# A decoder step on one core: side pieces held until a PSUM bank is free, memory attention in two passes over the tokens, a new order in the first stage

## The chip, the core and the metric

The kernel runs on one core of a Trainium2 chip. TensorE (PE in the profile) multiplies, VectorE (DVE) and ScalarE (ACT) work elementwise, GpSimd (POOL) does small copies and sums, SyncE (SP) issues the DMAs. The metric is the device time of one execution in microseconds, as a median over runs. A change of 0.2% is about 2.5 us here.

## What is computed

One layer of a hybrid decoder, for 512 prompt tokens and 8 x 4 = 32 sample tokens, 544 in all, with the same weights. Model width is 1024. Everything is kept transposed: a tile is 128 channels by 544 tokens.

```python
u = rmsnorm(h, norm_mix)
qa, ka, va, qkv_b, z_b, beta, a, gate_a, gate_b = split(u @ w_in)
o_a = dilated_attention(qa, ka, va, caches)        # three groups of 4 heads, keys by stride
o_b = gated_deltanet(qkv_b, z_b, beta, a, state)   # 8 heads of 128, a chain over chunks
h += (sigmoid(gate_a) * (o_a @ w_branch_a) + sigmoid(gate_b) * (o_b @ w_branch_b)) @ w_out
# memory attention: 4 heads of 128, 256 memory tokens; the sample tokens have caches of their own
q = rmsnorm(h, norm_mem_q) @ w_mem_q
h += softmax(q @ mem_k.T / sqrt(128)) @ mem_v @ w_mem_o
gate, up = split(rmsnorm(h, norm_ffn) @ w_up)
h += (silu(causal_dwconv3(gate) + b) * up) @ w_down
y = rmsnorm(h, norm_final)
```

The caches and states, shifted by the new tokens, are outputs too.

## The kernel before

**Dense blocks.** All weights are cut into blocks of 128 x 1024 floats (512 KB), in the order that `plan()` gives: `dq`, `dk`, `dv` (dilated attention), `z`, `gq`... (DeltaNet), `gb`, `ga` (gates), `mk`, `mv` (memory keys and values), then `wa` and `bb` (the two branches), `wo`, four `mq` (queries into the memory, one head each), four `mo`, and the FFN's `fg`, `fu`, `fd`. `load_to` loads a block into one of three buffers `wr`. `split_to` splits it into a high and a low part, `wh` by ACT and `wl` by DVE, in two buffers each, so that a block's split waits until the last block but one has been used. The tokens are split in the same manner (`xh`, `xl` in the first stage, then `uh`/`ul`, `obh`/`obl`, `nh`/`nl`, `oh`/`ol`). `dense` multiplies a block by eight such tiles: for each of eight slices k three products (`wh` by high, `wh` by low, `wl` by high), each as two matmuls of 272 tokens, into one of two wide PSUM tiles `pd`.

**Side pieces.** All other work (attention, the DeltaNet chain, convolutions, softmax) is written as Python generators, called streams, that use four small PSUM banks (`b`). After each slice k `dense` calls `tick`, which may put the next piece of a stream into the program at that place. There is one program order for each engine, and every engine works strictly in it: a piece whose input is late holds everything behind it on its engine. The builder keeps an account: estimated costs of every instruction, and from them a time at which each engine, tile and bank would be done. `tick` takes the stream of highest priority whose input is ready by the account. `need` and `drain` force pieces in where a dense block needs their result.

**The first stage.** `start` loads the first weight block, the parameters `par` and eight tiles `x`; ACT and DVE split each (`xh`, `xl`) and, in between, sum squares. `first` runs `dq` and `dk` on the unscaled tokens, then makes the tokens' RMS factor (`rstd`: matmuls with ones, a square root on ACT, a reciprocal on DVE; `spread`: matmuls that spread it over the partitions into `rx`), evacuates both products by DVE, and runs `dv`, while ACT and DVE make the scaled tokens `uh`, `ul`.

**Merge.** `merge` multiplies the dilated branch (`wa`) and then the DeltaNet branch (`bb`). The first two `bb` blocks are first run over heads 0 to 5, and then over heads 6 and 7, which come last out of the chain.

**Memory attention.** `cross` runs the four `mq` blocks over all 544 tokens. After each it adds a stream `cross_head` (scores of the prompt tokens, softmax, transposes, values), and writes `cross_keys` straight into the program: the sample tokens' scores against cached keys `mks`, summed in `csc`. After the last block `cross_sample` (softmax of `csc`, product with the cached values `mvs`) and what is left of the streams follow with no dense block between. `mem_out` then runs `mo`, and the FFN follows.

All calls reach the hardware through one helper, so every instruction has the same line in the profile (L329). Tiles tell the work apart.

Of the kernel before, what the change touches and what calls it, by code (L numbers as in the profile page):

```python
# [111 lines left out]
def plan():  # L112

    blocks = []
    for kind, k in MIX:
        if kind == "mem":
            blocks += [("mk", h) for h in range(4)] + [("mv", q) for q in range(4)]
            continue
        blocks += [(kind + c, k) for c in "qkv"] if kind in "gd" else [(kind, k)]
    blocks += [("wa", m) for m in range(2)] + [("bb", m) for m in range(8)]  # L120
    blocks += [("wo", m) for m in range(8)]
    blocks += [("mq", h) for h in range(4)]
    blocks += [("mo", q) for q in range(4)]
    for s in range(0, KF, SEC):
        for j in range(s, min(s + SEC, KF)):
            blocks += [("fg", j), ("fu", j)]
        blocks += [("fd", (s, m)) for m in range(8)]
    return blocks


def _layout(i):
# [10 lines left out]
    def blk(name, key):  # L142
# [22 lines left out]
        if name == "mq":  # L165
            return _tiles(wmq, [128 * key])[0]
# [70 lines left out]
class _View:  # L237
# [17 lines left out]
    def __getattr__(self, name):  # L255
        return getattr(self.raw, name)

# [135 lines left out]
class Builder:  # L393
# [123 lines left out]
    def split_to(self, j):  # L517
        while self.next_split <= min(j, len(self.plan) - 1):
# [8 lines left out]
            hi = self.wp.tile([128, c], F32R, name=f"wh{n}", tag="wh", bufs=NHL)  # L527
            lo = self.wp.tile([128, c], F32R, name=f"wl{n}", tag="wl", bufs=NHL)
            self.acc.rotate("wh", NHL, _key(hi))
            self.acc.rotate("wl", NHL, _key(lo))  # L530
# [3 lines left out]
            self.hl.pop(n - NHL, None)  # L534
# [98 lines left out]
    def tick(self):  # L633
# [4 lines left out]
        while c["PE"] - t0 < PE_SHARE:  # L638
            runs = self.runnable()
            for n in sorted(range(len(runs)), key=lambda n: (runs[n]["prio"], runs[n]["ready"])):  # L640
                st = runs[n]
                lag = max(c["V"], c["A"]) - c["PE"]
                if st["ready"] <= c["PE"] and self.room(st, [a + b for a, b in zip((MAIN, 0), self.older(runs, n))]) and lag < LAG[st["prio"]] and c["P"] - c["PE"] < 6.0:
# [77 lines left out]
    def start(self):  # L721
# [12 lines left out]
        x = [self.s(name="x") for _ in range(KD)]  # L734
        self.load(out=x[0], in_=I["xT"][:, 0, :])
        for k in range(1, KD):
            self.load(out=x[k], in_=I["xT"][:, k, :])
# [7 lines left out]
        def square(k):  # L745
# [4 lines left out]
        self.split_to(0)  # L750
        for k in range(KD):
            g = self.p("g_mix", k)
            xh.append(self.s(dt=F32R, name="xh")), xl.append(self.s(dt=F32R, name="xl"))
            self.split_scaled(x[k], g, xh[k], xl[k])
            if k == 7:
                self.split_to(1)
            if k % 2:
                square(k // 2)
        for k in range(KD // 2, KD):
            square(k)  # L760
        return x, list(zip(xh, xl)), acc

    def first(self, t, x, xs, acc):

# [4 lines left out]
        def stat(k):  # L769
            if k == 5:  # L770
                r5.append(self.rstd([acc], N))
            if k == 7:
                self.spread(r5[0], N, r)
        pk = self.dense(("dk", t), xs, each=stat)
        del acc
        tl = [self.dil_evac(t, 0, pq, r), self.dil_evac(t, 1, pk, r)]
        self.uh, self.ul = [], []
        us = {}
# [6 lines left out]
        scale(0)  # L785

        def chain(k):
            scale(k + 1)
            self.split_x(us.pop(k), self.uh, self.ul)
        ps = self.dense(("dv", t), xs, each=chain)  # L790
        del xs
        tl.append(self.dil_evac(t, 2, ps, r))
        self.dil_done(t, tl)
# [754 lines left out]
    def dil_tiles(self, t):  # L1548
        us = list(zip(self.uh, self.ul))
        self.dil_done(t, [self.dil_evac(t, kind, self.dense((name, t), us)) for kind, name in enumerate(("dq", "dk", "dv"))])  # L1550
# [129 lines left out]
    def dil_sample(self):  # L1680
# [109 lines left out]
        yield 1, 0, 2, 0  # L1790
# [32 lines left out]
        v.tensor_tensor(o, o, acc[:, None, :].to_broadcast([128, 2, 64]), OP.add)  # L1823
        yield from self.wait(("ap", 0), ("ap", 1))
# [26 lines left out]
    def merge(self):  # L1851
# [28 lines left out]
        for lo, hi in ((0, HFIRST), (HFIRST, 8)):  # L1880
            xs = heads(lo, hi)
            for m in range(2):
                ps[m] = self.dense(("bb", m), xs, k0=lo, ps=ps.get(m), start=lo == 0, stop=hi == 8, ahead=m == (hi == 8))
# [14 lines left out]
    def out_proj(self):  # L1898
# [10 lines left out]
        for m in range(8):  # L1909
# [9 lines left out]
            self.hstat(m, "g_mq")  # L1919
# [6 lines left out]
    def hstat(self, m, gain, eng=None):  # L1926
# [7 lines left out]
        if m < 7:  # L1934
# [8 lines left out]
        if m == 7:  # L1943
            split()


    def cross(self):
        nc = self.nc
        v, act, mm = nc.vector, nc.scalar.activation, nc.tensor.matmul
        ident = self.cst("ident")  # L1950
        xs = list(zip(self.nh, self.nl))
        self.oh, self.ol = [None] * 4, [None] * 4
        r = None
        for h in range(4):
            if r is None:
                r = []
                ps = self.dense(("mq", h), xs, mid=lambda: r.append(self.rstd([self.hacc], N)))
                r = self.spread(r[0], N, self.s(name="rq"))
            else:
                ps = self.dense(("mq", h), xs)  # L1960
                self.cross_keys(h - 1)
            q = self.s(name="cq")
            v.scalar_tensor_tensor(q, self.dv(ps), 128.0 ** -0.5, r, op0=OP.mult, op1=OP.mult)
            dst = self.qm[:, 0:4]
            dst = bass.AP(tensor=dst.tensor, offset=dst.offset + 264 * h, ap=[list(dst.ap[0]), [132, 2], [32, 4], [1, 4]])
            nc.gpsimd.tensor_copy(dst, q[:, 512:544].rearrange("p (c s j) -> p s c j", c=4, s=2))
            self.oh[h], self.ol[h] = self.s(dt=F32R, name="oh"), self.s(dt=F32R, name="ol")
            self.add(self.cross_head(h, q), 1, (3, 0), (4, 0))
            del q
        self.cross_keys(3)  # L1970
        self.cross_sample()
        self.drain()

    def cross_load(self, n):

        for e in range(n, n + 2):
# [3 lines left out]
            elif e < 16:  # L1980
                b = (0, 2, 4, 6, 1, 3, 5, 7)[e - 8]
                self.mvs[b] = self.l((128, 1024), name="mvs")
                self.load(out=self.mvs[b], in_=self.I["mvs"][b])

    def cross_begin(self):
# [4 lines left out]
        self.mks, self.mvs = {}, {}  # L1990
        self.cross_load(0), self.cross_load(2), self.cross_load(4)

    def cross_keys(self, h):
# [15 lines left out]
        self.cross_load(6 + 2 * h)  # L2009
# [14 lines left out]
    def cross_head(self, h, q):  # L2024
# [3 lines left out]
        pt = [self.s((128, 512), name="cpt") for _ in range(2)]  # L2028
        ps = []
        for i in range(2):  # L2030
            pb = self.bank()
            for e in range(2):
                mm(pb[:, 256 * e:256 * e + 256], q[:, 256 * i + 128 * e:256 * i + 128 * e + 128], self.mkT[h], start=True, stop=True)
            ps.append(self.soft(pb))
            if i == 0:
                yield "at", 0.0, (1, 0, 1, 0)
        del q
        yield 0, 0
        for i in range(2):
            p, pb = ps.pop(0), self.bank()  # L2040
            for e in range(2):
                for j in range(2):
                    nc.tensor.transpose(pb[:, 256 * e + 128 * j:256 * e + 128 * j + 128], p[:, 256 * j + 128 * e:256 * j + 128 * e + 128], ident)
            act(pt[0][:, 256 * i:256 * i + 256], pb[:, 0:256], AF.Copy)
            v.tensor_copy(pt[1][:, 256 * i:256 * i + 256], pb[:, 256:512])
            del p
        yield
        pb = self.bank()
        for e in range(2):
            mm(pb, self.mvT[e][:, 128 * h:128 * h + 128], pt[e], start=(e == 0), stop=(e == 1))  # L2050
        act(self.oh[h][:, 0:512], pb, AF.Copy)
        v.tensor_tensor(self.ol[h][:, 0:512], pb, self.oh[h][:, 0:512].bitcast(F32), OP.subtract)
        yield

    def cross_sample(self):
# [3 lines left out]
        mvs = self.mvs  # L2059
        p = self.soft(self.csc, 1)  # L2060
        self.csc = None
        self.tick()
# [5 lines left out]
        self.tick()  # L2068
        self.tick()

        po, ot = self.wide(), self.l((128, 1024), name="ot")
        for s in range(2):
            for e in range(2):
# [266 lines left out]
```

## Time and profile before

| | |
|---|---|
| median of 3 runs | 1270.43 us (1270.27 to 1271.31) |
| profiled execution | 1269.83 us, its span 1268.1 us |
| PE busy | 1222.2 us, 96% of the span |
| DVE, ACT, POOL busy | 709.4, 526.6, 160.9 us |
| mean granted TensorE clock | 0.988 |
| DMA | 233.56 MB, 184 GB/s mean |

The span runs from the first to the last instruction; 1.7 us of the time lie around it. PE is busy nearly all the time, so the questions are how long it is idle, where, and where its clock is lower than full. In rows of the timeline the columns are start, duration, engine, operation, tiles, shape, count, and in brackets the idle time before and what ended it. "x2" is a pair of matmuls; their durations overlap, so the pace is read from one start to the next.

### The profile page before, as it was taken

Reading aid. Unit: us, or ns where it says so; the run is one execution under the profiler, and the core shown is the slowest. Engines: PE = TensorE matmul, PEld = TensorE weight load, DVE = VectorE, ACT = ScalarE, POOL = GpSimd, SP = SyncE. Lnnn points to the kernel's source line nnn. Section 1 sums busy time; section 2 is a strip of 40 time slices with the busy share of each in tenths; the row PEclk is TensorE's granted clock in tenths of the full one; section 3 lists DMA queues with packets and bytes.
Section 4 is the critical chain, followed back from the end, with each engine's and each line's share of the span. In section 5 each row is a group of like instructions: output and inputs, shape, how many; then the busy total and the mean of one; then the engine's idle time right before and its main releaser. Section 6 shows DMA issues by size and latency. Waiting matters only on the chain.

```text
span 1268.1 us, 25946 instructions
## 1 busy us (share of the span) xinstructions
PE 1222.2 (96%) x10482; PEld 1165.2 (92%) x10482; DVE 709.4 (56%) x1343; ACT 526.6 (42%) x1115; POOL 160.9 (13%) x356
## 2 busy tenths in 40 slices
PE   7999999999999999998999999799999999999997
PEld 6899988899999988998799998499999999999997
DVE  6535346666767974486566555364553355434564
ACT  6334434555645533665642234254332233312341
POOL 0000100211152130020000000021210022101110
PEclk9999999999999998999998999899999999999998
DMA  6332774653576568656564483545555555555422
GB/s 224 95 122 79 279 265 155 214 174 100 178 267 215 200 215 295 199 190 193 175 219 143 166 325 110 191 171 186 193 187 183 183 189 206 203 184 183 157 83 71
DMA packets 90117, 233.56 MB, mean 184 GB/s; under 512 B 25865, under 2 KB 31478, under 8 KB 89221
## 3 DMA queue, kind: packets, MB, share of 16 engines
q1 hardware_dynamic: 89998, 231.90, 53.1%
q8 instruction: 83, 1.36, 0.4%
q14 instruction: 36, 0.29, 0.1%
HBM read 198.42 MB, written 77.58 MB: 218 GB/s over the span
## 4 chain that ended last, share of the span: by engine, by line
PE 71%; DVE 5%; ACT 2%; issue 2%; DMA 1%; POOL 0%; DVEq 0%; POOLq 0%; SPq 0%; ACTq 0%
PE pd L329 58%; PE b L329 13%; DVE wl L329 1%; DVE y L329 1%; ACT wh L329 1%; DMA qk<-park 0%; DVE xr L329 0%; DMA ft<-park 0%; DVE sz L329 0%; DVE m L329 0%; DMA mvs<-in_mvs 0%; DVE st L329 0%; DMA z<-park 0%; ACT hsq L329 0%; DVE su L329 0%
## 5 line engine op out<-in xcount | busy, mean ns | idle before, releaser
L329 DVE TENSOR_TENSOR wl<-wr,wh 128x1024 fp32r<-128x1024 f32 (+2 forms) x174 | 212.4, 1223 | 225.2 <-ACT wh L329 219.1
L329 ACT ACTIVATE wh<-wr 128x1024 fp32r<-128x1024 f32 (+2 forms) x174 | 177.1, 1021 | 122.7 <-PE pd L329 120.5
L329 PE MATMUL pd<-uh,wh 128*128 128x272 f32 x1024 | 223.5, 300 | 0.0
L329 PE MATMUL pd<-ul,wh 128*128 128x272 f32 x1024 | 212.7, 289 | 0.4 <-DVE ul L329 0.3
L329 PE MATMUL pd<-uh,wl 128*128 128x272 f32 x1024 | 212.3, 288 | 0.0
L329 PEld LDWEIGHTS pd<-uh,wh 128*128 128x128 f32 x1024 | 160.2, 189 | 7.7 <-issue 6.4
L329 PEld LDWEIGHTS pd<-ul,wh 128*128 128x128 f32 x1024 | 162.1, 189 | 0.9 <-DVE ul L329 0.8
L329 PE MATMUL pd<-nh,wh 128*128 128x272 f32 x768 | 161.6, 291 | 0.5 <-DVE xr L329 0.5
L329 PEld LDWEIGHTS pd<-uh,wl 128*128 128x128 f32 x1024 | 161.8, 188 | 0.0
L329 PE MATMUL pd<-nh,wl 128*128 128x272 f32 x768 | 159.4, 288 | 0.0
L329 PE MATMUL pd<-nl,wh 128*128 128x272 f32 x768 | 159.3, 288 | 0.0
L329 PEld LDWEIGHTS pd<-nh,wh 128*128 128x128 f32 x768 | 121.9, 188 | 2.3 <-issue 2.0
L329 PEld LDWEIGHTS pd<-nl,wh 128*128 128x128 f32 x768 | 121.7, 188 | 0.0
L329 PEld LDWEIGHTS pd<-nh,wl 128*128 128x128 f32 x768 | 121.6, 188 | 0.0
L329 POOL TENSOR_TENSOR sr<-fy,rf 128x512 f32<-128x512 f32 (+1 forms) x44 | 53.5, 1237 | 69.5 <-ACT fy L329 66.3
L329 DVE SCALAR_TENSOR_TENSOR y<-cb,par,y 128x568 f32<-128x568 f32 x72 | 58.9, 820 | 2.9 <-ACT y L329 1.1
L329 PE MATMUL pd<-fh,wh 128*128 128x272 f32 x256 | 53.2, 288 | 0.0
L329 PE MATMUL pd<-fl,wh 128*128 128x272 f32 x256 | 53.1, 288 | 0.0
L329 PE MATMUL pd<-fh,wl 128*128 128x272 f32 x256 | 53.1, 288 | 0.0
L329 DVE SCALAR_TENSOR_TENSOR fy<-fcb,par,fy 128x560 f32<-128x560 f32 x44 | 35.3, 802 | 22.4 <-ACT fy L329 21.7
L329 PEld LDWEIGHTS pd<-fh,wl 128*128 128x128 f32 x256 | 40.6, 188 | 0.0
L329 PEld LDWEIGHTS pd<-fh,wh 128*128 128x128 f32 x256 | 40.5, 188 | 0.0
(371 smaller groups left out, 2121.0 us busy)
## 6 DMA issues: line engine op xcount, KB each, us to landing
wr<-in_w SPq DMA_DIRECT2D x145, 512.0 KB
out_d<-in_c SPq DMA_DIRECT2D x32, 1022.0 KB
ft<-park SPq DMA_DIRECT2D x40, 256.0 KB
kc<-in_ck SPq DMA_DIRECT2D x18, 512.0 KB
kc<-in_cv SPq DMA_DIRECT2D x18, 512.0 KB
wr<-in_wd SPq DMA_DIRECT2D x16, 512.0 KB
out_d<-in_c SPq DMA_DIRECT2D x8, 1016.0 KB
park<-y SPq DMA_DIRECT2D x24, 256.0 KB
```

The source lines that it names most:

```text
L329: return f(*a, **k)
```

## The change

1. `tick` starts a piece only when, by the account, the bank that it will take is free as well.
2. Memory attention goes in two passes over the tokens: first tokens 256 to 543 (288, with the sample tokens) for all four heads, then tokens 0 to 255. `part` runs one block over such a range. Blocks `mq` 0 and 1 are loaded and split a second time (as `mq` 4 and 5). `cross_head` works on 256 tokens at a time; `cross_keys` and `cross_sample` become one stream with priority 0, so that its pieces too lie between dense slices; `mo` begins with the second range for two output tiles.
3. The first stage: `x` 0 is loaded first and the first weight block in two halves; squares come after all splits; `dv` goes into two small banks; `rstd` comes after `dk`, `spread` after two slices of `dv`, and a fourth block (`dq` of tile 2) still runs on the unscaled tokens.
4. `merge` splits a third `bb` block ahead, into two large slots; before the last `wo` tile's statistics the second `mq` block is split; two pieces of the sample attention end where DVE has work to do (`yield "at", self.acc.done`).

The core of the diff:

```diff
@@ tick
-                if st["ready"] <= c["PE"] and self.room(...) and ...:
+                if max(st["ready"], self.acc.last.get(self.ring["b"][-4], 0.0) - 0.0 if len(self.ring["b"]) >= 4 else 0.0) <= c["PE"] and self.room(...) and ...:
@@ start
-        self.load_to(0)
+        x = [self.s(name="x") for _ in range(KD)]
+        w0 = [self.s((128, 512), name="w0") for _ in range(2)]
+        self.load(out=x[0], in_=I["xT"][:, 0, :])
         self.load(out=self.par, in_=I["par"])
+        for e in range(2):
+            self.load(out=w0[e], in_=self.src[0][:, 512 * e:512 * e + 512])
+            for k in range(2 * e + 1, 5 * e + 3):
+                self.load(out=x[k], in_=I["xT"][:, k, :])
...
+        piece(0)
+        for k in range(KD):
...
+            self.split_scaled(x[k], g, xh[k], xl[k])
+            if k == 2:
+                piece(1)
+        self.split_to(1)
+        for k in range(KD):
             sq = self.s(name="xsq") if k else acc
             act(sq, x[k], AF.Square)
@@ first
         def stat(k):
-            if k == 5:
+            if k == 7:
                 r5.append(self.rstd([acc], N))
-            if k == 7:
-                self.spread(r5[0], N, r)
         pk = self.dense(("dk", t), xs, each=stat)
...
+            if k == 1:
+                self.spread(r5[0], N, r)
+                tl.append(self.dil_evac(t, 0, pq, r))
+                tl.append(self.dil_evac(t, 1, pk, r))
+                scale(0)
...
+        pv = [self.bank((128, NH)) for _ in range(2)]
...
+        p2 = self.dense(("dq", t2), xs, each=more)
@@ merge
-                ps[m] = self.dense(("bb", m), xs, ..., ahead=m == (hi == 8))
+                ps[m] = self.dense(("bb", m), xs, ..., ahead=lo == 0 or m == 1)
@@ new
+    def part(self, b, xs, ps, cols, k0=0, ahead=True, last=True, mid=None):
+        self.reserve(2)
+        hi, lo = self.weights(b, ahead)
+        for k, (xh, xl) in enumerate(xs):
+            w = slice((k0 + k) * 128, (k0 + k + 1) * 128)
+            for n, (w, x) in enumerate(((hi[:, w], xh), (hi[:, w], xl), (lo[:, w], xh))):
+                self.nc.tensor.matmul(ps, w, x[:, cols], ...)
+            if mid and k == len(xs) - 3:
+                mid()
+            if k % 2:
+                self.tick()
@@ cross
-            self.add(self.cross_head(h, q), 1, (3, 0), (4, 0))
-        self.cross_keys(3)
-        self.cross_sample()
-        self.drain()
+        self.add(self.cross_sample(), 0, (0, 0), (3, 0))
...
+        for h in range(4):
+            half = self.bank((128, 288)) if h < 2 else self.wide()[:, 0:288]
+            self.part(("mq", h), xs, half, slice(256, N), ...)
+            todo.append((h, half))
+            if h == 1:
+                r[0] = self.spread(r[0], N, self.s(name="rq"))
+            while h and todo:
+                evac(*todo.pop(0))
+        for n, h in enumerate((2, 3, 0, 1)):
+            half = self.wide()[:, 0:256] if n < 3 else self.bank((128, 256))
+            self.part(("mq", h + 4 if h < 2 else h), xs, half, slice(0, 256), ahead=n > 0)
+            query(h, 0, half)
@@ cross_sample (now with yields between its pieces)
+        for h in range(4):
+            yield from self.wait(("cq", h))
+            yield from self.on(self.mks[2 * h], self.mks[2 * h + 1], need=(2 if h == 3 else 0, 0))
+            self.cross_keys(h)
+            yield 1, 0, 3, 0
...
+            yield from self.on(*[x for c in range(4) for x in mvs[2 * c + s]])
@@ mem_out
+        ps = [self.wide() for _ in range(2)]
+        for i in (1, 0):
+            self.need(*[("oh", h, i) for h in range(4)], *[("os", 0)] * i)
+            for m in range(2):
+                self.part(("mo", 0), xs, ps[m][:, 512:800] if i else ps[m][:, 256:512], ...)
```

What it moves, at three places. Names are tiles with running numbers, and x4 is a count of equal instructions.

The first place is the start of the program. SyncE's queue of loads before, and then after the change (`w_91` and `w_92` are the two halves of the first weight block that `wr_83` was):

```order
L329 DMA wr_83<-in_w 128x1024
L329 DMA par<-in_par 128x293
L329 DMA x_87<-in_xT 128x544
L329 DMA x_88<-in_xT 128x544
L329 DMA x_89<-in_xT 128x544
```

```order
L339 DMA x_83<-in_xT 128x544
L339 DMA par<-in_par 128x293
L339 DMA w_91<-in_w 128x512
L339 DMA x_84<-in_xT 128x544
L339 DMA x_85<-in_xT 128x544
L339 DMA w_92<-in_w 128x512
L339 DMA x_86<-in_xT 128x544
```

The first token tile and half a block now come ahead of the other half. Later in the same stage, on PE, where `spread` stands (`b_303`, `b_309` before; `b_329`, `b_335` after), between the last matmuls of `dk` (`pd_243`) and the first of `dv` (`pd_327`) before:

```order
L329 MATMUL pd_243<-xh_151,wl_158 128x272 x2
L329 MATMUL b_303<-ident,m_288 128x128 x4
L329 MATMUL b_309<-ident,m_288 128x32
L329 MATMUL pd_327<-xh_116,wh_239 128x272 x2
L329 MATMUL pd_327<-xl_117,wh_239 128x272 x2
```

and inside `dv` (now in the banks `b_315` and `b_316`) after:

```order
L339 MATMUL b_316<-xl_121,wh_245 128x272
L339 MATMUL b_315<-xh_120,wl_246 128x272
L339 MATMUL b_316<-xh_120,wl_246 128x272
L339 MATMUL b_329<-ident,m_306 128x128 x4
L339 MATMUL b_335<-ident,m_306 128x32
L339 MATMUL b_315<-xh_124,wh_245 128x272
```

`dv` no longer takes the wide tile that `dq`'s product still holds.

The second place is the merge, on PE: the last transposes of the DeltaNet heads (`b<-ident,ft`) against the products of heads 6 and 7. Before, heads 6 and 7 of the first `bb` block (`pd_8766`) follow the transposes at once:

```order
L329 MATMUL pd_8816<-obh_8756,wh_8762 128x272 x2
L329 MATMUL pd_8816<-obl_8757,wh_8762 128x272 x2
L329 MATMUL pd_8816<-obh_8756,wl_8763 128x272 x2
L329 MATMUL b_8883<-ident,ft_8445 128x128 x4
L329 MATMUL b_8894<-ident,ft_8555 128x128 x4
L329 MATMUL pd_8766<-obh_8901,wh_8640 128x272 x2
L329 MATMUL pd_8766<-obl_8902,wh_8640 128x272 x2
```

After, the first of the two transposes stands ahead of the second `bb` block (`pd_8865`), and the other stands four slices later:

```order
L339 MATMUL pd_8808<-obh_8777,wl_8744 128x272 x2
L339 MATMUL b_8853<-ident,ft_8402 128x128 x4
L339 MATMUL pd_8865<-obh_8274,wh_8804 128x272 x2
L339 MATMUL pd_8865<-obl_8275,wh_8804 128x272 x2
L339 MATMUL pd_8865<-obh_8274,wl_8805 128x272 x2
```

The chain that feeds these transposes ended among the `bb` blocks before; it now ends among the `wa` blocks.

The third place is the end of the memory attention, on PE (`cq` are queries, `mkv` the memory keys and values, `cp` softmax rows, `cpt` their transposes, `ot` the sample result). Before, after the 16 products with `mvs`:

```order
L329 MATMUL b_10376<-mkv_9600,cq_10307 128x256 x2
L329 MATMUL pd_10388<-ident,ot_10353 128x128 x8
L329 MATMUL b_10405<-cpt_10211,mkv_9601 128x512
L329 MATMUL b_10405<-cpt_10212,mkv_9602 128x512
L329 MATMUL b_10410<-ident,cp_10345 128x128 x4
L329 MATMUL b_10417<-ident,cp_10381 128x128 x4
L329 MATMUL b_10424<-cpt_10338,mkv_9601 128x512
L329 MATMUL b_10424<-cpt_10339,mkv_9602 128x512
L329 MATMUL pd_10435<-oh_9956,wh_10200 128x272 x2
```

After, between the second range of `mo` (the first row) and its first range (the last rows):

```order
L339 MATMUL pd_10455<-oh_10134,wl_10400 128x288
L339 MATMUL b_10480<-cpt_10437,mkv_9608 128x256
L339 MATMUL b_10480<-cpt_10437,mkv_9609 128x256
L339 MATMUL b_10485<-ident,cp_10445 128x128 x4
L339 MATMUL b_10493<-mkv_9606,cq_10452 128x256 x2
L339 MATMUL b_10505<-cpt_10490,mkv_9608 128x256
L339 MATMUL b_10505<-cpt_10490,mkv_9609 128x256
L339 MATMUL b_10510<-ident,cp_10498 128x128 x4
L339 MATMUL b_10518<-cpt_10515,mkv_9608 128x256
L339 MATMUL b_10518<-cpt_10515,mkv_9609 128x256
L339 MATMUL pd_10454<-oh_9970,wh_10399 128x256
L339 MATMUL pd_10454<-ol_9971,wh_10399 128x256
```

The products with `mvs` have moved ahead, in between the slices of the second `mq` pass; the scores of the last head, their softmax and the two products behind them still follow each other here.

More of the change, by code (lines that the diff above doesn't have):

```diff
@@ L121, in plan @@
     blocks += [("wo", m) for m in range(8)]
-    blocks += [("mq", h) for h in range(4)]
+    blocks += [("mq", h) for h in range(6)]
     blocks += [("mo", q) for q in range(4)]
@@ L165, in blk @@
         if name == "mq":
[L166 removed]
+            return _tiles(wmq, [128 * (key % 4)])[0]
         if name == "mo":
@@ L784, in scale, with more @@
                 x[k] = None
-        scale(0)
         def chain(k):
-            scale(k + 1)
-            self.split_x(us.pop(k), self.uh, self.ul)
-        ps = self.dense(("dv", t), xs, each=chain)
+            if k == 1:
[3 more added lines that the diff above has]
+                scale(0)
+            elif k % 2:
+                scale(k // 2)
+                self.split_x(us.pop(k // 2 - 1), self.uh, self.ul)
+        hi, lo = self.weights(("dv", t))
+        pv = [self.bank((128, NH)) for _ in range(2)]
+        for k in range(KD):
+            w = slice(128 * k, 128 * k + 128)
+            for n, (w, x_) in enumerate(((hi[:, w], xs[k][0]), (hi[:, w], xs[k][1]), (lo[:, w], xs[k][0]))):
+                for e in range(2):
+                    nc.tensor.matmul(pv[e], w, x_[:, NH * e:NH * e + NH], start=(k == 0 and n == 0), stop=(k == KD - 1 and n == 2))
+            chain(k)
+        dv = self.s(name="dv")
+        for e in range(2):
+            nc.vector.tensor_tensor(dv[:, NH * e:NH * e + NH], pv[e], r[:, NH * e:NH * e + NH], OP.mult)
+        self.store(out=self.O["dkv"][1, t], in_=dv[:, 0:512])
+        tl.append(dv)
+        del pv, dv
+        self.dil_done(t, tl)
+        t2 = t + 2
+        def more(k):
+            if k < 5:
+                e = 3 + k
+                scale(e + 1)
+                self.split_x(us.pop(e), self.uh, self.ul)
+        p2 = self.dense(("dq", t2), xs, each=more)
         del xs
-        tl.append(self.dil_evac(t, 2, ps, r))
-        self.dil_done(t, tl)
+        return self.dil_evac(t2, 0, p2, r)
     def mem_stream(self):
@@ L1546, in sample_bias, with dil_tiles @@
         return t
-    def dil_tiles(self, t):
+    def dil_tiles(self, t, q=None):
         us = list(zip(self.uh, self.ul))
-        self.dil_done(t, [self.dil_evac(t, kind, self.dense((name, t), us)) for kind, name in enumerate(("dq", "dk", "dv"))])
+        tl = [q] if q is not None else []
+        for kind, name in list(enumerate(("dq", "dk", "dv")))[len(tl):]:
+            tl.append(self.dil_evac(t, kind, self.dense((name, t), us)))
+        self.dil_done(t, tl)
     def dil_evac(self, t, kind, ps, r=None):
@@ L1882, in merge @@
             for m in range(2):
-                ps[m] = self.dense(("bb", m), xs, k0=lo, ps=ps.get(m), start=lo == 0, stop=hi == 8, ahead=m == (hi == 8))
+                ps[m] = self.dense(("bb", m), xs, k0=lo, ps=ps.get(m), start=lo == 0, stop=hi == 8, ahead=lo == 0 or m == 1)
         obs = heads(0, 8)
@@ L1947, in cross @@
     def cross(self):
-        nc = self.nc
-        v, act, mm = nc.vector, nc.scalar.activation, nc.tensor.matmul
-        ident = self.cst("ident")
+        v = self.nc.vector
         xs = list(zip(self.nh, self.nl))
         self.oh, self.ol = [None] * 4, [None] * 4
[L1953 to L1963, printed above, removed]
+        self.add(self.cross_sample(), 0, (0, 0), (3, 0))
@@ new lines, in query @@
+        def query(h, i, ps):
+            q = self.s((128, 256), name="cq")
+            v.scalar_tensor_tensor(q, ps[:, 0:256], 128.0 ** -0.5, r[0][:, 256 * i:256 * i + 256], op0=OP.mult, op1=OP.mult)
+            self.add(self.cross_head(h, i, q), 1, (2, 0), (2, 0))
+        todo = []
+        for h in range(4):
+            half = self.bank((128, 288)) if h < 2 else self.wide()[:, 0:288]
+            self.part(("mq", h), xs, half, slice(256, N), ahead=h < 3, mid=(lambda: r.append(self.rstd([self.hacc], N))) if h == 1 else None)
+            todo.append((h, half))
[3 more added lines that the diff above has]
+                evac(*todo.pop(0))
```

203 lines of the change are left out of this document (117 added, 86 removed).

## The prediction

> **What bounds the kernel now.** I read the page first, then busy time by stage, then what PE waited for, then single rows.
>
> ```profile
> span 1268.1 us, 25946 instructions
> PE 1222.2 (96%) x10482; PEld 1165.2 (92%) x10482; DVE 709.4 (56%) x1343; ACT 526.6 (42%) x1115; POOL 160.9 (13%) x356
> PE 71%; DVE 5%; ACT 2%; issue 2%; DMA 1%; POOL 0%; DVEq 0%; POOLq 0%; SPq 0%; ACTq 0%
> ```
>
> PE carries the span and 71% of the chain that ended last. The change removes no PE work: by the program's order it issues the same products, in other shapes. So only two things can move the time: PE's idle time, 1268.1 - 1222.2 = 45.9 us, and time in which PE works at a lower clock. Busy time by stage (columns: stretch, length, busy time and count of PE, PEld, DVE, ACT, POOL, granted clock, DMA share, GB/s):
>
> ```profile
> 0.00:39.20 39.20, 29.32 (x208) 28.09 (x208) 28.21 (x43) 23.41 (x35) 0.62 (x6) 1.00 0.52 185
> 39.20:560.00 520.80, 512.25 (x4880) 481.50 (x4879) 312.83 (x716) 250.20 (x637) 78.16 (x197) 0.99 0.58 195
> 560.00:670.00 110.00, 100.59 (x902) 92.41 (x901) 71.29 (x171) 59.69 (x161) 7.54 (x11) 0.97 0.58 192
> 759.20:825.40 66.20, 57.76 (x399) 42.80 (x398) 29.80 (x66) 22.69 (x62) 1.77 (x4) 0.95 0.45 166
> 825.40:850.90 25.50, 25.12 (x194) 24.46 (x192) 15.98 (x18) 12.18 (x17) 6.91 (x5) 1.00 0.41 151
> 850.90:1220.00 369.10, 368.86 (x2915) 368.89 (x2915) 175.33 (x214) 115.60 (x136) 65.86 (x133) 1.00 0.52 184
> ```
>
> The last row is the FFN: PE is busy in all of it, so nothing is to be had there. The idle time lies in the first stage (9.9 us), in the DeltaNet phase (8.6), from the memory keys to the merge (9.4) and in the memory attention, `mq` to `mo` (8.4 + 0.4). What PE waited for, in total, times and longest:
>
> ```profile
> PE pd L329 <- ACT xh L329: 7.4, 1, 7.4
> PE b L329 <- DVE sz L329: 2.8, 6, 0.8
> PE b L329 <- DVE cp L329: 2.3, 1, 2.3
> PE b L329 <- DVE ft L329: 2.0, 1, 2.0
> PE b L329 <- DVE ssc L329: 1.9, 1, 1.9
> PE pd L329 <- DVE dq L329: 1.9, 1, 1.9
> PE b L329 <- ACT cpt L329: 1.7, 1, 1.7
> PE pd L329 <- DMA mvs<-in_mvs: 1.7, 1, 1.7
> PE b L329 <- POOL qm L329: 1.4, 1, 1.4
> PE pd L329 <- DVE obl L329: 1.3, 1, 1.3
> PE b L329 <- DVE so L329: 0.8, 1, 0.8
> ```
>
> Each is a wait of one or two microseconds at a place where a piece follows too soon on what it needs. They cost more than their length. Four stretches around such places, and pairs of matmuls shortly after the merge's waits and later:
>
> ```profile
> 468.00:485.00 17.00, 13.60 (x159) 9.72 (x159) 10.66 (x19) 2.34 (x10) 2.58 (x3) 0.84 0.73 227
> 668.00:680.00 12.00, 11.23 (x69) 10.98 (x70) 7.63 (x11) 3.98 (x5) 0.00 (x0) 0.75 0.30 106
> 800.00:807.00 7.00, 3.24 (x41) 1.75 (x40) 3.27 (x8) 1.69 (x5) 0.21 (x1) 1.00 0.75 237
> 807.00:814.00 7.00, 5.03 (x25) 0.83 (x23) 1.48 (x4) 1.66 (x6) 0.00 (x0) 0.75 0.63 235
> ...
> 669.85 0.66 PE L329 MATMUL pd<-obh,wh 128*128 128x272 f32 x2
> 670.30 0.65 PE L329 MATMUL pd<-obl,wh 128*128 128x272 f32 x2
> 674.41 0.42 PE L329 MATMUL pd<-obl,wh 128*128 128x272 f32 x2
> 674.66 0.41 PE L329 MATMUL pd<-obh,wl 128*128 128x272 f32 x2
> ```
>
> After the merge's waits a pair takes 0.45 us (669.85 to 670.30), later 0.25 (674.41 to 674.66). The granted clock says the same: 0.75 over 12 us is 3.0 us of clock lost. In the memory attention PE is busy for 3.24 of 7 us, and the clock of the next 7 us is 0.75; over `mq` to the last side piece 0.95 of 66.2 us is 3.3 us lost. Around 476 us it is 0.16 x 17 = 2.7.
>
> The Trainium skill ("TensorE: Matmul & The Clock Gate", "What's actually happening") puts the return to the half clock after at least one idle window of about 3.4 us. The longest single wait after the start is 2.3 us here, and the clock fell all the same; the trace decides, and by that rule alone the waits would bring their own length and no more, which is a rival below.
>
> **The change, part by part.** The sum is made against the profiled execution, 1269.83 us, of which the span is 1268.1; the median of the runs, 1270.43, stands 0.6 above it.
>
> *First stage.* Rows of ACT, PE and DVE:
>
> ```profile
> 4.41 1.06 ACT L329 ACTIVATE wh<-wr 128x1024 fp32r<-128x1024 f32 x1 [2.18 <-DMA wr<-in_w]
> 6.58 0.75 ACT L329 ACTIVATE xh<-x,par 128x544 fp32r<-128x544 f32 x1 [1.12 <-DMA x<-in_xT]
> 7.38 0.82 PE L329 MATMUL pd<-xh,wh 128*128 128x272 f32 x2 [7.38 <-ACT xh L329]
> 25.25 1.19 DVE L329 SCALAR_TENSOR_TENSOR dq<-pd,rx 128x512 f32<-128x512 f32 x2 [2.63 <-ACT rx L329]
> 26.59 0.49 PE L329 MATMUL pd<-xh,wh 128*128 128x272 f32 x2 [1.86 <-DVE dq L329]
> ```
>
> The block (512 KB) lands at 4.41, `par` and `x` 0 (147 + 272 KB) at 6.58: 193 KB per us. The new order needs 272 + 147 + 256 = 675 KB before PE can begin, at 4.41 + 163/193 = 5.25 us; half a split (0.53) and 0.80 from the split of `x` 0 to PE give 6.6 instead of 7.38: -0.8. The wait of 1.86 us for `dq`'s evacuation goes, since `dv` has banks of its own: -1.9. Of the other 0.6 us of idle time half: -0.3. What takes its place is DVE, on which the evacuations and the chain of `u` follow each other; its first reader is now a block later, 24 pairs x 0.25 = 6.1 us, which covers it. The extra store and the same number of squares lie beside PE. Sum -3; bounds -4 (no idle time after the start) and -1 (the evacuation's wait only moves).
>
> *Pieces that wait for data.* The two new yields let dense slices run while DVE finishes `ssc` and `so`: 1.9 + 0.8 = 2.7 us, of which I take -2.4; bounds -2.7 and 0.
>
> *The bank rule.* Its price does not appear in the trace of before; the nearest rows are the waits for `sz` (2.8 us in 6), in which pieces `b` stand behind DVE's reading of banks, with the clock lost there (2.7): 5.5 us at most. The account's times are estimates, so some waits stay: -3; bounds -5.5 and +3 (a rule that makes pieces later can add waits of the same kind).
>
> *Merge.* The waits for `ft` and `obl` (3.3 us) and the clock lost behind them (3.0) are 6.3 us. In the new order four slices of dense work stand between the last transposes and the products of heads 6 and 7, and the DeltaNet chain ends earlier. Late next is the split of those heads on ACT and DVE: -5; bounds -6.3 and 0. The third block split ahead costs PE nothing.
>
> *Memory attention.* Idle time 8.4 + 0.4 and clock lost 3.3: 12.1 us at most. Nearly all sits in the part without a dense block between (800 to 825 us), which the new order dissolves into the second pass. Two blocks are split twice: 1.06 us of ACT each (the `wh` row) and as much of DVE, hidden, since both engines are busy for less than half of this stage (29.80 and 22.69 of 66.2). The slices of 288 and 256 tokens are the same sum of columns. What stays is the last head's chain, which in the order has almost nothing beside it:
>
> ```profile
> L329 DVE TENSOR_REDUCE m<-b 128x2 f32<-128x512 f32 x8 | 5.5, 688 | 3.3 <-PE b L329 3.2
> L329 DVE TENSOR_SCALAR cp<-cp,m 128x256 f32<-128x256 f32 x17 | 5.3, 351 | 0.4
> L329 ACT ACTIVATE cp<-b,m 128x256 f32<-128x256 f32 x16 | 7.5, 470 | 20.4 <-DVE m L329 20.4
> L329 ACT ACTIVATE cpt<-b 128x256 f32<-128x256 f32 x9 | 3.4, 387 | 4.7 <-PE b L329 4.5
> ```
>
> Reduce 0.69, two exponentials 0.94, two scalings 0.70 and some 0.6 for the reciprocal and the handing over are 2.9 us, less one product of about 0.8 beside them: 2.1. Then 0.5 for the copies and 0.5 for the high and low parts: 3.1. With about 1 us for the start of the first pass (its splits now come every 3.3 us) 4.1 stay: -8. Bounds -12 and -2 (the waits find new places, and the tail's gap of 2 us costs a cold window).
>
> *New waits elsewhere.* All pieces from 39 to 670 us lie in other places than before: +2; bounds 0 and +6.
>
> Sum: -3 - 2.4 - 3 - 5 - 8 + 2 = -19.4, so 1269.83 - 19.4 = 1250.4, and against the median 1251.
>
> **Rivals.** *The memory attention keeps its waits.* For: the forced tail, and the last four `mvs` tiles (2 MB) that are loaded only when head 3's keys are used. At 237 GB/s (800 to 807 us) they take 9 us, and in the order about 9 us of PE work stand before their use. Then this term is -2 instead of -8, perhaps the merge half: 1256 to 1264.
>
> *Only the waits' own length comes back,* by the skill's window: the clock's share of my terms is 3.3 (memory attention), 2.5 (merge) and 1.2 (bank rule), 7 us: 1258.
>
> *Slower: the bank rule starves the DeltaNet chain.* A piece turned away waits for the next slice, 3 pairs or 0.76 us. The second group has two heads in series, 4 chunks with 3 dependent pieces each, 24 pieces. One slice lost by each is 18 us, which the merge would wait for, and eats the gain; two are 36 us: 1287. It decides at more than 25 lost slices in series. Against it: in the new order the chain ends among the `wa` blocks instead of the `bb` blocks, so it has gained on the dense work.
>
> *The change does nothing,* as every wait is replaced by its like: 1268 to 1273. Against it: the first stage's wait and the part without dense blocks go by construction.
>
> **How the numbers follow.** Forecast (1243 to 1256): 0.57. Memory attention keeps its waits (1256 to 1264): 0.19. Waits' length only (around 1258): 0.09. More than forecast, below 1243: 0.05. No change: 0.05. Slower: 0.05. The range 1243 to 1264 takes in the first three, 0.85. 0.2% is 2.5 us, about what a measurement tells from no change: faster 0.90, same 0.05, slower 0.05.
>
> **What would show it.** First stage: PE starts near 6.6 us and never waits for `dq`. Data waits: `ssc` and `so` gone from PE's waits. Merge: no wait over 1 us for `ft` or `obl`, and a clock of 1.00 behind it. Memory attention: from the first `mq` matmul to the first `fg` 84 us instead of 91.7, one wait near 2 us for the last `cp`. Bank rule: `sz` below 1.5 us. In all, PE idle near 34 us and a mean clock above 0.988. It is wrong if the waits for `cp`, `cpt` and `mvs` return in the second pass, or if PE waits for `St` and `xc` grow.

## The result and the profile after

The changed kernel took 1251.10 us (median; 1247.10 to 1252.14) against 1270.37 us before; ratio 0.984, interval 0.982 to 0.986. The forecast was 1251. The profiled execution of the changed kernel is its shortest, 1247.1 us; a second one is shown with the first experiment. The page after:

```profile
span 1245.3 us, 26010 instructions
PE 1212.5 (97%) x10498; PEld 1164.3 (93%) x10498; DVE 716.3 (58%) x1360; ACT 529.1 (42%) x1126; POOL 160.5 (13%) x352
PE 88%; DVE 4%; ACT 3%; DMA 3%; issue 1%; SPq 1%; POOL 0%; POOLq 0%; DVEq 0%; ACTq 0%
```

PE's idle time fell from 45.9 to 1245.3 - 1212.5 = 32.8 us, and PE's busy time by 1222.2 - 1212.5 = 9.7 us, with 16 more products: the same work at a higher clock. By the clock records of the traces, PE ran at half clock for seven intervals of 3.41 us before and for two after, four in the second execution shown below (besides a last one at the end of the program). Half of 3.41 us is 1.7, so the five intervals fewer are 8.5 of the 9.7 us. Busy time by stage, with the stages cut at the same work: the first stage (one block longer than before, since the fourth block on unscaled tokens was moved into it), the phase up to the last gate block, gates to merge, `wo`, memory attention with `mo`, and the FFN. First before, then after (columns: stretch, length, busy time and count of PE, PEld, DVE, ACT, POOL, granted clock, DMA share, GB/s):

```profile
39.20:580.90 541.70, 531.63 (x5035) 500.65 (x5034) 329.99 (x761) 260.82 (x663) 85.69 (x208) 0.99 0.57 191
580.90:710.60 129.70, 121.82 (x1051) 113.61 (x1051) 77.72 (x153) 60.44 (x150) 0.00 (x0) 0.96 0.56 188
710.60:759.20 48.60, 48.60 (x386) 48.60 (x385) 26.37 (x31) 17.34 (x23) 0.00 (x0) 1.00 0.68 245
759.20:851.10 91.90, 82.88 (x592) 67.27 (x590) 45.88 (x84) 34.94 (x80) 8.69 (x9) 0.96 0.44 161
```

```profile
0.00:42.80 42.80, 35.17 (x257) 33.62 (x258) 32.01 (x49) 24.56 (x37) 1.32 (x7) 1.00 0.54 188
42.80:578.40 535.60, 526.98 (x5108) 496.93 (x5107) 337.02 (x780) 263.66 (x673) 86.47 (x208) 1.00 0.59 196
578.40:696.10 117.70, 113.92 (x928) 108.60 (x927) 70.72 (x131) 55.52 (x136) 0.00 (x0) 0.97 0.57 190
696.10:744.80 48.70, 48.70 (x387) 48.70 (x385) 26.38 (x31) 17.36 (x24) 0.00 (x0) 1.00 0.68 246
744.80:828.40 83.60, 79.89 (x609) 69.54 (x607) 48.90 (x99) 38.39 (x91) 6.87 (x5) 1.00 0.57 202
828.40:1195.40 367.00, 367.00 (x2900) 367.00 (x2901) 174.05 (x212) 115.05 (x135) 65.21 (x133) 1.00 0.52 182
```

Memory attention with `mo` went from 91.9 to 83.6 us. The stretch from the gates to the merge went from 129.7 to 117.7 us, and before it has 123 more products (1051 against 928): there side pieces of the DeltaNet chain still stood in it that now have run earlier. `wo` and FFN are as long as before. By these rows the 22.8 us between the two profiled executions are 2.5 up to the last gate block, 12.0 from the gates to the merge and 8.3 in the memory attention. What PE waited for, after (some of the view's rows):

```profile
PE pd L339 <- ACT xh L339: 7.3, 1, 7.3
PE b L339 <- DVE m L339: 3.2, 3, 2.5
PE b L339 <- DVE St L339: 2.3, 1, 2.3
PE b L339 <- DVE y L339: 2.0, 1, 2.0
PE b L339 <- DVE cp L339: 1.6, 1, 1.6
PE b L339 <- DVE sz L339: 1.0, 2, 0.7
PE b L339 <- DVE ft L339: 0.5, 1, 0.5
PE b L339 <- ACT cpt L339: 0.5, 1, 0.5
PE pd L339 <- ACT obh L339: 0.4, 1, 0.4
```

`dq`, `ssc`, `so`, `mvs`, `qm` and `obl` are gone. `y` is new, and `m` (0.5 us before) and `St` (0.4 us) have grown.

### The profile page after: what moved, and what is told of

Its sections match the earlier page's. It is cut to its first block, busy times and chain, and to the rows that moved or that the text cites. A ratio compares the mean times of both kernels' runs of the same rounds, so it can differ in the third digit from the quotient of the medians.

```text
span 1245.3 us, 26010 instructions
## 1 busy us (share of the span) xinstructions
PE 1212.5 (97%) x10498; PEld 1164.3 (93%) x10498; DVE 716.3 (58%) x1360; ACT 529.1 (42%) x1126; POOL 160.5 (13%) x352
## 4 chain that ended last, share of the span: by engine, by line
PE 88%; DVE 4%; ACT 3%; DMA 3%; issue 1%; SPq 1%; POOL 0%; POOLq 0%; DVEq 0%; ACTq 0%
PE pd L339 70%; PE b L339 19%; DVE wl L339 1%; DMA usol<-su 1%; ACT wh L339 1%; DMA z<-park 1%; SPq L339 1%; DMA U<-usol 1%; DVE xr L339 0%; DMA ft<-park 0%; DMA w<-in_w 0%; DVE Dm L339 0%; DVE y L339 0%; ACT m L339 0%; ACT hsq L339 0%
## 5 line engine op out<-in xcount | busy, mean ns | idle before, releaser
L339 PE MATMUL pd<-uh,wl 128*128 128x272 f32 x1008 | 208.5, 288 | 0.5 <-DVE wl L339 0.5
L339 PE MATMUL pd<-ul,wh 128*128 128x272 f32 x1008 | 208.5, 288 | 0.0
L339 PEld LDWEIGHTS pd<-uh,wh 128*128 128x128 f32 x1008 | 157.2, 189 | 8.3 <-issue 6.6
L339 PE MATMUL pd<-nh,wh 128*128 128x272 f32 (+2 forms) x744 | 159.2, 291 | 0.5 <-DVE xr L339 0.5
L339 PEld LDWEIGHTS pd<-uh,wl 128*128 128x128 f32 x1008 | 158.8, 188 | 0.7 <-DVE wl L339 0.7
L339 PEld LDWEIGHTS pd<-ul,wh 128*128 128x128 f32 x1008 | 159.1, 188 | 0.0
L339 PE MATMUL pd<-nl,wh 128*128 128x272 f32 (+2 forms) x744 | 157.7, 288 | 0.0
L339 PE MATMUL pd<-nh,wl 128*128 128x272 f32 (+2 forms) x744 | 157.6, 288 | 0.0
L339 POOL TENSOR_TENSOR hacc<-hacc,hsq 128x544 f32<-128x544 f32 x6 | 8.2, 1373 | 260.9 <-ACT hsq L339 260.9
L339 PEld LDWEIGHTS pd<-fl,wh 128*128 128x128 f32 x256 | 40.6, 188 | 0.0
```

The costliest lines, as they stand in the source:

```text
L339: return f(*a, **k)
```

## The experiments

The runs fall into three groups, in this order. Beside them the kernel before took 1270.9, 1269.9 and 1270.4 us (medians), so a difference of 1 us between runs of two groups says little.

**The same kernel again.** No edit.

> The changed kernel once more, for a second profile: the profiled execution took 1247.1 us, the other three 1250.7 to 1252.1. Theory A (the clock): the same waits fall differently against the clock's intervals of 3.41 us, each half-clock interval costing about 1.7 us; a profile near 1251 shows two or three more such intervals, and PE idle time near 33 us as before. Theory B (the data): the executions differ in what PE waits for (DMA landings); then idle time is 3 to 5 us higher and the count of half-clock intervals the same.

1251.36 us; the profiled execution had a span of 1249.7 and PE busy for 1216.4 us, so 33.3 us of idle time, against 32.8 in the span of 1245.3. The same two stretches of the program, first in the shorter execution, then in this one:

```profile
359.00:366.00 7.00, 4.99 (x43) 4.81 (x42) 7.00 (x12) 4.44 (x15) 5.67 (x5) 1.00 0.48 144
584.40:605.00 20.60, 17.68 (x193) 15.86 (x194) 9.89 (x21) 12.02 (x36) 0.00 (x0) 0.83 0.33 113
```

```profile
361.60:368.60 7.00, 5.00 (x31) 4.81 (x29) 7.00 (x12) 3.60 (x12) 4.83 (x5) 0.76 0.60 198
586.80:607.40 20.60, 17.68 (x171) 15.88 (x170) 9.75 (x20) 11.75 (x35) 0.00 (x0) 0.75 0.34 116
```

In the first rows PE waits 2.0 us for `y` and is busy for 5.0 of 7 us in both; behind it the clock stayed at 1.00 once and was 0.76 the other time. Theory A holds: the clock accounts for 7 x 0.24 + 20.6 x 0.08 = 3.3 of the 4.4 us, the later start of PE (8.1 against 7.3 us) for 0.8.

**Without the bank rule.**

```diff
-  if max(st["ready"], self.acc.last.get(self.ring["b"][-4], 0.0) - 0.0 ...) <= c["PE"] and ...
+  if st["ready"] <= c["PE"] and ...
```

> The changed kernel with the old condition in tick; all other parts of the change stay. Theory A (the prediction's term): the rule is worth 3 us, so 1254, and the waits for sz come back near 2.8 us. Theory B: the rule carries most of the 12 us that lie between the first stage and the memory attention, the edits of the merge and the yields following it: 1260 to 1263. Theory C: the rule is worth nothing or costs (it only moves pieces): 1248 to 1251.

1263.98 us, ratio 0.995 (0.993 to 0.996): 12.6 us back, theory B. But `sz` is the least of it (3.1 us of waits, against 1.0 in the changed kernel). The loss sits from the gates to the merge, in the same work as the stretch of 117.7 us after:

```profile
583.40:712.50 129.10, 117.94 (x940) 110.18 (x939) 74.69 (x145) 57.76 (x140) 0.00 (x0) 0.97 0.54 185
```

11.2 us idle there instead of 3.8, in waits for `ft`, `U`, `obl`: the chain is late at the merge again, as the row of its products `b<-xc,U` tells (shortest, median and longest duration in ns, then first and last start; before, after, and without the rule):

```profile
L329 PE MATMUL b<-xc,U x48: 270/275/377, 507.5 to 659.7; 128*128 128x128 f32 x48
```

```profile
L339 PE MATMUL b<-xc,U x48: 270/275/377, 482.2 to 641.6; 128*128 128x128 f32 x48
```

```profile
L339 PE MATMUL b<-xc,U x48: 270/275/377, 506.6 to 662.8; 128*128 128x128 f32 x48
```

**With the old memory attention.** `cross`, `cross_head`, `cross_keys`, `cross_sample`, `cross_load`, `cross_begin`, `mem_out`, `hstat` and `out_proj` as before, and four `mq` blocks.

> The changed kernel with the memory attention of before (one pass, the sample attention behind it without dense work, mo as before). Theory A: the part brings its idle time and the clock behind it, 8 us: 1259. Theory B: only the waits' own length, 4.5 to 5 us: 1256. Theory C: the two passes bring more than their stage, since the side pieces left over from the merge now also find dense work: 1262 or more.

1257.92 us, 6.6 us more than the changed kernel run beside it, between A and B. Its stage, which the changed kernel does in 83.6 us:

```profile
746.10:839.40 93.30, 84.17 (x593) 67.89 (x591) 45.86 (x84) 34.99 (x80) 8.68 (x9) 0.95 0.44 159
```

9.1 us of idle time and 0.05 x 93.3 = 4.7 us of clock, against 3.7 and none. By this profile the stage is worth 9.7 us, by the medians 6.6. The profiled executions of this run and of the one beside it both lie at their medians, and the difference is found ahead of the stage: this one reaches it at 746.1 instead of 748.9 us, since PE happened to start at 6.8 instead of 8.1 us and the clock did not fall behind `y`.

**With the old first stage.** `start`, `first` and `dil_tiles` as before.

> The changed kernel with the first stage of before. PE's first product starts at 7.3 us in both, so of the predicted 3 us only the wait for dq's evacuation and smaller ones are left, 2.5 us by the start of the scaled tokens' blocks. Theory A: 2.5 us come back: 1253.5. Theory B: the DeltaNet chain and its waits take up the lead later, nothing comes back: 1251. The order of all later side pieces shifts too, by which 3 us either way can come in.

1253.53 us, 2.2 us more: the size of theory A, but the times overlap (1251.46 to 1254.45, against 1249.99 to 1252.60). The trace is clearer: the wait for `dq` is back, with 1.8 us.

**The rule alone, and the yields alone,** on the kernel before. The edits are the line of `tick` above, and in the sample attention:

```diff
-        yield 1, 0, 2, 0
+        yield "at", self.acc.done, (1, 0, 2, 0)
...
+        yield "at", self.acc.done, (0, 0, 0, 0)
```

> The kernel before with the bank rule as its only change. Without the rule the changed kernel took 12.6 us more. Theory A (the rule needs the two new yields): by the program's order, 975 products of side pieces stand ahead of the sixtieth block of weights with the rule alone, against 1032 before and 1095 in the changed kernel; the chain is not earlier at the merge, so 1267 to 1273. Theory B (the rule by itself is worth its 12 us): 1258.

> The kernel before with the two new yields as its only change. Theory A: the yields take away the waits for ssc and so, 2.7 us, and the chain stands at 1008 products ahead of the sixtieth block, no earlier than before (1032): 1267 to 1269. Theory B (the yields carry what the rule seemed to bring): 1258 to 1262.

1281.22 us, ratio 1.009 (1.008 to 1.010), and 1278.55 us, ratio 1.007 (1.006 to 1.008). Both make the kernel before slower, the rule by 11.3 us and the yields by 8.7 us, both beyond what theory A expected. With the yields the waits for `ssc` and `so` are gone, and others took their place.

**The changed kernel without the yields.**

> The changed kernel without the two yields; rule and all else stay. Theory A (the rule needs the yields): as with the rule left out, the chain is late at the merge (975 products ahead of the sixtieth block against 1095): 1261 to 1266, and the waits for ssc and so come back. Theory B (each part stands by itself): 2.4 us come back, 1253.5.

1269.99 us, 18.6 us back, more than theory A expected: the whole gain of the change. From the gates to the merge it now takes 152.7 us, with 15.2 us idle and a clock of 0.90, and the chain's products run from 533 to 671 us:

```profile
567.40:720.10 152.70, 137.50 (x1122) 127.56 (x1122) 91.19 (x189) 70.99 (x191) 7.43 (x11) 0.90 0.53 173
```

```profile
L339 PE MATMUL b<-xc,U x48: 270/275/580, 533.2 to 670.6; 128*128 128x128 f32 x48
```

**With the old merge.** `EXTRA` empty, and `ahead` as before.

> The changed kernel with the blocks of the merge split ahead as before (no third block ahead, no large slots for it). Theory A: the chain ends ahead of the merge's heads 6 and 7 by the rule and the yields, the third block is worth nothing more: 1250 to 1252. Theory B (the prediction's term): 5 us come back, 1256.

1252.35 us, 1.0 us more, which is no more than the difference between two groups: the third block split ahead is worth little. In the merge there is then a wait of 1.4 us for `ft`.

**Rule and yields together,** on the kernel before.

> The kernel before with the bank rule and the two yields, and nothing else of the change. Alone they cost 11.3 and 8.7 us. Theory A (they work only together: 1095 products of side pieces stand ahead of the sixtieth block of weights, no piece of a stream has to be forced in between 380 and 700 us; 69 are with the rule alone, 23 with the yields alone): the changed kernel's 1251 plus what the other parts brought (2.2 first stage, 6.6 memory attention, 1.0 merge), 1261. Theory B (each has its own cost or gain, and the other parts of the change turned them): slower than before, 1275 or more.

1263.14 us, ratio 0.995 (0.994 to 0.996): 7.3 us faster, where each alone is slower. Theory A, with a gain 2 us smaller than expected.

**Holding a piece 0.05 us longer.** By the account, that is; the changed kernel otherwise.

```diff
-  self.acc.last.get(self.ring["b"][-4], 0.0) - 0.0
+  self.acc.last.get(self.ring["b"][-4], 0.0) + 0.05
```

> The changed kernel, in which the rule holds a piece 0.05 us longer by the account. Theory A (what counts is which order the rule happens to give; with this margin 975 products stand ahead of the sixtieth block and 43 pieces are forced): 1264 to 1272, like the kernels without the rule or without the yields. Theory B (the rule spares waits for banks; 0.05 us changes nothing): 1250 to 1253.

1273.78 us, ratio 1.003 (1.002 to 1.004): 22 us slower than with a margin of 0, and slower than the kernel before. Waits longer than any that the two kernels had for these tiles:

```profile
PE b L339 <- DVE m L339: 8.5, 3, 4.9
PE pd L339 <- ACT wh L339: 2.9, 1, 2.9
```

**The memory tokens' RMS sums half a block earlier.**

```diff
-  if h == 1 and k == 0:
+  if h == 0 and k == 4:
       self.rtok = self.rstd([self.macc], 256)
```

> The changed kernel, in which the sums for the memory tokens' RMS factor are made half a block earlier (after slice 4 of the first mk block instead of slice 0 of the second), so that ACT's table load, its split of a weight block, the root and the reciprocal end before PE spreads the factor. The order ahead of 570 us stays as it is. This takes away PE's longest wait after the start, 2.5 us for m. Theory A (the wait also costs the clock behind it: two or three intervals of 3.41 us at half clock, 1.7 us each): 1244.5 to 1246, and no half-clock interval between 585 and 605 us. Theory B (only its own length): 1248.5 to 1249.

1243.96 us, ratio 0.980 (0.979 to 0.981): 7.3 us below the mean of the two medians of the changed kernel, for a wait of 2.5 us, and the times do not overlap (1242.39 to 1246.58, against 1247.10 to 1252.60). This run beats both kernels. The two stretches shown with the first experiment, here:

```profile
361.00:368.00 7.00, 5.00 (x43) 4.81 (x42) 7.00 (x12) 4.45 (x15) 5.68 (x5) 1.00 0.47 148
586.00:606.60 20.60, 19.88 (x239) 18.08 (x238) 13.67 (x30) 15.51 (x48) 0.00 (x0) 1.00 0.39 138
```

239 products instead of 171 or 193 are done in the same 20.6 us, at full clock. Theory A, and slightly more than its span. The whole stretch from the gates to the merge:

```profile
579.90:692.20 112.30, 110.64 (x929) 105.79 (x928) 70.52 (x131) 55.42 (x136) 0.00 (x0) 1.00 0.60 199
```

It is 5.4 us shorter than in the first execution of the changed kernel (117.7) and 6.5 shorter than in the second (118.8): 2.1 us less idle time, and two or three intervals less at half clock. The rest of the 7.3 us may be chance: `y` (5.00 of 7 us) cost no clock in this execution, for one.

**And token tile 0 split first.**

```diff
-  piece(0)
   for k in range(KD):
       ...
-      if k == 2:
-          piece(1)
+      if k in (0, 2):
+          piece(k // 2)
```

> As the kernel with the earlier RMS sums, and ACT splits token tile 0 ahead of the first half block, not behind it. x 0 and par are asked for ahead of the half block; if they land earlier, PE starts 0.5 to 0.6 us sooner (Theory A), 0.5 us below the kernel without this edit. Theory B: x 0, par and the half block land together and PE waits for whichever split is last: no difference.

1243.36 us (1243.14 to 1244.48), 0.6 us below the kernel without this edit (1242.39 to 1246.58): the sign and size of theory A, but the times overlap. The timeline is clearer. After, then with this edit:

```profile
6.00 0.63 ACT L339 ACTIVATE w<-w 128x512 fp32r<-128x512 f32 x1 [3.77 <-DMA w<-in_w]
7.32 0.82 PE L339 MATMUL pd<-xh,w 128*128 128x272 f32 x2 [7.32 <-ACT xh L339]
```

```profile
4.01 0.75 ACT L339 ACTIVATE xh<-x,par 128x544 fp32r<-128x544 f32 x1 [1.78 <-DMA par<-in_par]
6.16 0.63 ACT L339 ACTIVATE w<-w 128x512 fp32r<-128x512 f32 x1 [1.40 <-DMA w<-in_w]
6.84 0.82 PE L339 MATMUL pd<-xh,w 128*128 128x272 f32 x2 [6.84 <-ACT w L339]
```

PE starts 0.68 us after the half block's split begins instead of 1.32. The half block lands 2.1 us behind `par`; it is what PE waits for.

## Why the prediction came out, and where it was wrong

The time was right to 0.1 us, the working was not. By its terms:

*First stage,* -3 forecast, -2.2 measured. The wait for `dq` went, as forecast. PE's start did not move to 6.6 us: it was 7.3 and 8.1. The step that failed is the landing time (5.25 us, from 193 KB per us): the half block landed at 6.00 and 6.79 us, and from there to PE it took 1.32 us, as in the working (0.53 + 0.80). The term of 0.8 us was also smaller than what one execution differs from another: over all traces PE starts at 6.8 to 8.1 us with this new order of loads, and at 6.5 to 7.6 with the old.

*Data waits and bank rule,* -2.4 and -3, as two things with prices of their own. The waits themselves went as forecast: `ssc` and `so` are gone, and `sz` fell from 2.8 to 1.0 us. But they are not what the two edits are worth, and that is the largest error of the working. Each alone costs the kernel before 8.7 and 11.3 us, together they gain 7.3 us; taken out of the changed kernel, the one costs 18.6 and the other 12.6 us. What they change is the order. The table sets beside each measured time two numbers of the program: the products outside the dense blocks that stand ahead of the last product of the sixtieth block of weights, and the pieces that `need` and `reserve` forced in ahead of 700 us by the account because a dense block needed their result or their slots. The third number is from the traces: when the chain's last product `b<-xc,U` starts.

| kernel | products | forced | chain's last product at, us | us |
|---|---|---|---|---|
| before | 1032 | 14 | 659.7 | 1270 |
| before + yields | 1008 | 23 | 667.3 | 1278.6 |
| before + rule | 975 | 69 | 667.5 | 1281.2 |
| before + both | 1095 | 0 | 648.8 | 1263.1 |
| changed, no rule | 1008 | 23 | 662.8 | 1264.0 |
| changed, no yields | 975 | 69 | 670.6 | 1270.0 |
| changed, hold 0.05 us longer | 975 | 43 | 670.4 | 1273.8 |
| changed | 1095 | 0 | 641.6 and 645.8 | 1251 |

In each base the order in which the chain stands furthest ahead, with nothing forced, is the fastest, and the later the chain ends, the longer the kernel takes. Only the two orders with 975 products on the changed base, whose chains end together, stand the other way about by what was forced. The kernels on the before base have the old memory attention, first stage and merge, worth 6.6 + 2.2 + 1.0 us; within a base the rest is due to order. The row with 0.05 us shows that the idea of the rule (spare PE the wait for a bank) is not what pays: the same rule, 0.05 us stricter, brings the waits for `sz` down to 0.4 us and gives an order that loses the whole gain. That the change hit a good order was not to be known from the profile of before; it could be read from the order after, and the prediction did read there that the chain ends among the `wa` blocks. It priced that with the merge instead.

*The slower rival* (the bank rule starves the chain, 1287) was given 0.05. For the rule alone the outcome came near: 1281.2 us, with a chain that starts 26 us later than before and ends 8 us later:

```profile
L329 PE MATMUL b<-xc,U x48: 270/275/580, 533.2 to 667.5; 128*128 128x128 f32 x48
```

That this comes from slices lost one by one, as the rival has it, was not shown; the yields alone, without the rule, also make the chain late. That the two together do the opposite is what it did not think of.

*Merge,* -5. Its waits for `ft` and `obl` (2.0 and 1.3 us) and the half clock behind them went, as the chain is early; with the rule, the yields and the old merge one wait of 1.4 us for `ft` is left. The new order of the merge takes away that one, and brings 1.0 us by the medians.

*Memory attention,* -8, measured 6.6 by medians when it alone is undone, 9.7 by its stage in that run, and 8.3 by its stage before and after the whole change. The stage took 83.6 us (84 forecast), with one wait of 1.6 us for the last `cp` (2 forecast). `mvs` was not waited for.

*New waits,* +2. There is one whose removal gave 7.3 us: `m`, the memory tokens' RMS factor. Its sums are `b<-ones,macc`, its use is `b<-ident,m`. Before, then after:

```profile
586.42 0.50 PE L329 MATMUL b<-ones,macc 128*128 128x1 f32 x4
587.31 0.44 PE L329 MATMUL b<-U,ft 32*32 32x32 f32 x16
587.68 0.66 PE L329 MATMUL b<-ident,ft 128*128 128x128 f32 x4
588.27 0.44 PE L329 MATMUL b<-U,ft 32*32 32x32 f32 x16
590.09 1.05 PE L329 MATMUL b<-ident,m 128*128 128x128 f32 x4
586.39 1.28 ACT L329 ACT_TABLE_LOAD   x1
```

```profile
583.88 0.61 PE L339 MATMUL b<-ones,macc 128*128 128x1 f32 x4
588.18 1.22 PE L339 MATMUL b<-ident,m 128*128 128x128 f32 x4 [2.52 <-DVE m L339]
585.32 1.04 ACT L339 ACTIVATE wh<-wr 128x1024 fp32r<-128x1024 f32 x1
586.37 1.28 ACT L339 ACT_TABLE_LOAD   x1
```

Before, PE had waited 0.9 and 0.8 us for a block's split just ahead of the sums, so that ACT's table load (of the table for the square root) began with them, and three pieces of the chain stood between the sums and their use. Now there is neither: the chain is further ahead in the order (it still runs until 641.6 us), and nothing covers ACT's weight split and table load. The prediction said for each edit what hides it, but did not ask what the chain's pieces, once they are gone from their places, had been hiding. It had named a growing wait for `St` as a sign that it is wrong. That wait did grow, from 0.4 to 2.3 us, at 549 us, and the clock did not fall behind it in either execution; the other signs (`cp`, `cpt`, `mvs`, `xc`) stayed away.

*Only the waits' own length comes back* is refuted: 2.5 us of wait taken away gave 7.3 us.

*The list of idle time* in the prediction comes to 36.7 of the 45.9 us. It leaves out 9.0 us behind the FFN, in the last 48 us of the program; the change did not touch them.

So the errors cancel inside one sum, and that the total came out to 0.1 us is luck. Forecast were -5.4 for rule and yields, -5 for the merge and +2 for new waits, -8.4. Measured were -7.3 for the pair and -1.0 for the merge, -8.3, and the pair's figure holds the new wait for `m` already (its kernel waits 2.5 us there too). If that costs there what it costs in the changed kernel, 7.3, the early chain by itself brings 14.6 us. All single terms, by their medians, add up to 7.3 + 1.0 + 2.2 + 6.6 = 17.1 of 19.3 us; the other 2.2 were not located. Why just this pair of edits gives the early chain was not settled either: it was followed in the order, not derived.

## What to carry to other kernels

In a program order that is built by a greedy rule, do not price an edit of the rule by the wait that it is meant to spare: build the order and see how far the critical chain stands at some fixed block and what had to be forced. Undo such edits one by one and in pairs before you believe in any of them; an edit that loses 11 us alone can be half of a gain. When pieces of a chain move to other places, look for what they had been covering.

## What the runs showed of the hardware

In the clock records of the traces the clock is at half for one or more whole intervals of 3.41 us, and in each trace all of these lie on one grid of that step. What counts is the share of one grid interval in which PE is busy. Over all intervals at full clock in the fourteen traces, without the first 20 us and the end of each program, the next interval was at half clock in 26 of 26 cases with a share below 0.45, in 15 of 44 with 0.45 to 0.65, and in 2 of 4898 with more.

The same wait of 2.0 us for `y` shows what this means. In the second execution of the changed kernel it lay wholly inside one interval (share 0.41), and the clock fell. In the run with the earlier RMS sums it lay across a border (0.66), and in the first execution of the changed kernel 0.2 us of it lay beyond the border (0.48); there the clock stayed at 1.00. Where the grid lies differs from one execution to the next, so the same wait costs only its length in one and 1.7 us more for each half-clock interval in another. Of the 4.4 us between the two profiled executions of the changed kernel the clock makes 3.3. Behind the wait for `m` the fall lasted two or three intervals, although PE was busy for 0.7 to 1.0 of the intervals at half clock that came ahead of another; why is open.

The Trainium skill ("TensorE: Matmul & The Clock Gate", "What's actually happening") tells of a free-running window of 3413 ns; the traces agree. It puts the fall of the clock after at least one idle window; the traces differ, since PE was busy for at least 0.14 of every interval ahead of a fall.
